# A hybrid conv block on one core: the first norm's squares shared by ScalarE and VectorE, its sum taken on TensorE in four parts, with zero matmuls between

## The chip, the cores and the metric

The kernel runs on one core of a Trainium2 chip. The metric is the device time of one execution in microseconds (us). A core has five queues that run side by side and wait for each other by semaphores: TensorE (PE, matmuls; its weight loads are shown as PEld), VectorE (DVE), ScalarE (ACT), GpSimd (POOL) and SyncE (SP, which here only issues DMAs).

## The reference

One layer on x of 1024 positions by 1024 channels, float32. A small vector c sets scales and shifts:

```python
mod = jax.nn.silu(c) @ w_ada[l] + b_ada[l]
sh1, sc1, g1, sh2, sc2, g2 = jnp.split(mod[:, None, :], N_MOD, axis=-1)
h = rms_norm(x, norm_mix_g[l]) * (1.0 + sc1) + sh1
proj = jnp.einsum('bsd,de->bse', h, w_in[l])
```

`rms_norm` divides by the root of the mean square over the channels. The projection feeds a short gated convolution and a 31-tap convolution module; their gated sum goes through one more matrix and is added to x; a second norm with its own modulation and a SwiGLU layer follow, then a last norm. The change touches only what comes before the first matmuls of `proj`: the squares, their sum, the root, and the first columns of `mod`.

## The kernel before, in words

Channels lie on the 128 partitions, positions along the free axis; 1024 channels are 8 chunks (k = 0 to 7), 1024 positions are 2 halves (h) of 512. A matmul multiplies a 128x128 block of weights with a 128x512 tile. Most products are made of float32r operands split in a high and a low part, so that one product is three matmuls: L286 (high weights, high operand), L287 (high weights, low operand), L289 (low weights, high operand), all in `mm3`. In the lead's first half, chunks 0 to 2 are multiplied whole in float32 instead (L282): the profile shows such a matmul as two records.

The lead is the part up to the end of the first seven columns of blocks of `proj` (`LEAD = 7`):

- SyncE loads x's first half as four tiles of two chunks (L442), then `ada` tiles (columns of w_ada, L266) and the weights `w_first` in the order of use. ScalarE's queue loads c and the vector of constants `vec`.
- c is spread over the partitions by two one-row matmuls (`cb`, L447); ScalarE's Silu of them is `cs` (L451).
- `squares_x` squares the eight chunks on ScalarE (L397) and adds them in a chain on VectorE (L401). `norm_start` sums over the partitions with one matmul by ones (`ss`, L407), and ScalarE takes an approximate reciprocal root (`rx0r`, L336). `rstd_end` sharpens it with three VectorE instructions, a Newton step (L341 to L343).
- `modulation(i)` makes one column of `mod` for one block of channels: a VectorE product of an `ada` tile with `cs`, summed along the row (L267). `affine` makes a scale from it (`aff`, L273).
- `modulate` multiplies a chunk with its scale and the norm (L353, VectorE); ScalarE adds the shift (L357, or L361 for a high part such as `h30h`: chunk 3, half 0), VectorE makes the low part (L362, `h30l`).
- `act_x(k, h)` calls these for a chunk and a half; `row_blocks` multiplies each chunk into seven PSUM tiles `lead`. In the second half (h = 1) the same is done with x's other half: its squares and their sum (`rx_1`) are made while chunks 6 and 7 of the first half are multiplied.
- Weights are split by a cast on ScalarE (`wh`, L208) and a subtraction on VectorE (`wl`, L209). There are three `wh` and three `wl` buffers, taken in turn, so a cast waits for the last matmul that reads the weights three casts earlier.
- `glu` and `gate` read the first half's seven `lead` tiles out of PSUM: ScalarE's Sigmoid (`sig`, L426 and L431) and VectorE's product (`u`, L427). The second half's tiles take the banks over as these come free.

The order on each queue is made by a scheduler from the code's order; `tc.issue_after(ins)` tells it to place what follows behind `ins`. After the lead come nine stages that the change does not touch.

Of the kernel before, what the change touches and what calls it, by code (L numbers as in the profile page):

```python
# [39 lines left out]
P = 128  # L40
# [7 lines left out]
CK = 31  # L48
# [62 lines left out]
def block_kernel(ctx: ExitStack, tc: tile.TileContext, x0, xT, c, vecs, ada, w_first, w_plain, w_duals,  # L111
# [35 lines left out]
    def hl_tile(name, dt=F32R):  # L147
        return tp.tile([P, H], dt, tag="t", name=name)
# [7 lines left out]
    def f32(t):  # L156
        return t.bitcast(F32)
# [102 lines left out]
    def modulation(i, raw=None):  # L260

        b = ADA_ORDER[i]
        if raw is None:
            raw = load(ada[i])
        else:
            nc.sync.dma_start(raw, ada[i])  # L266
        nc.vector.tensor_tensor_reduce(  # L267
            out=raw, in0=raw, in1=cs, scale=1.0, scalar=col(V_ADA, b),
            op0=ALU.mult, op1=ALU.add, accum_out=modc(b),
        )  # L270

    def affine(dst, k, sc, g):
        nc.vector.scalar_tensor_tensor(  # L273
# [119 lines left out]
    def squares_x(src, acc=None):  # L393

        for t in src:
            sq = g_tile("sq")
            act = nc.scalar.activation(sq, t, AF.Square, scale=1.0 / 32.0)  # L397
            if acc is None:
                acc = sq
            else:  # L400
                add = nc.vector.tensor_tensor(acc, acc, sq, ALU.add)  # L401
        squares_x.ins = act.ins, add.ins
        return acc
# [36 lines left out]
    for k in range(0, KC, 2):  # L440
        t = uc_tile("x0", T)
        nc.sync.dma_start(t, x0[k // 2])  # L442
        xin[k], xin[k + 1] = (t[:, s] for s in halves)
    cb = []
    for s in halves:
        cb.append(ps_tile("cb"))
        nc.tensor.matmul(cb[-1], ones[:1], crow[:, s], start=True, stop=True)  # L447
    acc = squares_x([xin[k] for k in range(KC)])
    with tc.issue_after(squares_x.ins[0]):
        for s, t in zip(halves, cb):  # L450
            silu = nc.scalar.activation(cs[:, s], t, AF.Silu)  # L451
    load_rsqrt(silu.ins)
    rx_0 = rstd_end(*norm_start(acc, "rx0"))

    def lead_w(k):
        if k < WHOLE:
# [3 lines left out]
    def act_x(k, h):  # L460
        nonlocal rx_1
        if h == 0:
            with ExitStack() as after:
                after.enter_context(tc.issue_after(modulate.ins[0] if k else squares_x.ins[1]))
                for i in range(2 * k, 2 * k + 2):
                    modulation(i, ucp.tile([P, T + CK - 1], F32, tag="uc", name="ada")[:, :D])
            affine(aff1, k, 8, V_GMIX)
            x[k, 0] = s_tile(f"x{k}0")
        whole = h == 0 and k < WHOLE
        hT[k][h] = modulate(x[k, h], rx_1 if h else rx_0, aff1[:, k : k + 1], modc(k),  # L470
                            None if whole else f"h{k}{h}", None if h else xin[k])
        if h == 0:
            if k == X1_AT:
                for i in range(KC):
                    x[i, 1] = s_tile(f"x{i}1")
                    nc.sync.dma_start(x[i, 1], xT[i, :, halves[1]])
            elif k == X1_AT + 1:
                with tc.issue_after(modulate.ins[2]):
                    rx_1 = squares_x([x[i, 1] for i in range(KC)])
                with tc.issue_after(mm3.ins), tc.issue_after(modulate.ins[1]):  # L480
                    rx_1 = norm_start(rx_1, "rx1", ss_tile=ps2_tile)
            elif k == KC - 1:
                with tc.issue_after(modulate.ins[2]):
                    rx_1 = rstd_end(*rx_1)
            if whole:
                return x[k, 0]
        elif k < WHOLE:
            hT[k][0] = split(x[k, 0], hl_tile, f"h{k}0")
        return hT[k][h]
# [733 lines left out]
```

## Time and profile before

| | |
|---|---|
| runs | 1496.49, 1498.00, 1498.34 us; median 1498.0 |
| profiled execution | 1498.83 us, of which the span of its instructions is 1497.1 |
| busy in the span | PE 1467.0, DVE 1140.8, ACT 623.8, POOL 537.7 us |
| first lead matmul (L282) | at 18.72 us |
| second half of the lead (L286 with h01h) | from 63.78 us |

Busy time is summed over the instructions of an engine. In the views, "a <-b" behind a time names what the engine waited for before it. Records of consecutive matmuls overlap by some 0.16 us, so their spacing, not their duration, is what one costs.

### The profile page before, as it was taken

To read this page: it belongs to the slowest core of one execution; us is meant where nothing else is said; L and a number is where in the kernel's file an instruction comes from. 1 tells how busy PE (TensorE), PEld (TensorE's weight loads), DVE (VectorE), ACT (ScalarE), POOL (GpSimd) and SP (SyncE) were. 2 spreads that over 40 slices of the span, in tenths; PEclk is the share of its full clock that TensorE was granted. 3 is DMA by queue.
4 is the path that set the end of the run, shared out by engine and by line. 5 is a ranking of instruction groups with operands and counts; after the bars stand their busy time and mean duration, and the time that the engine had idled before them with its cause. 6 is when DMAs were issued, how large, how long until landed. Compare 5 with 4: busy or idle time off the path is not lost.

```text
span 1497.1 us, 17720 instructions
## 1 busy us (share of the span) xinstructions
PE 1467.0 (98%) x6455; PEld 1201.2 (80%) x6455; DVE 1140.8 (76%) x1569; ACT 623.8 (42%) x896; POOL 537.7 (36%) x467
## 2 busy tenths in 40 slices
PE   6999999999999999999999999999999999999997
PEld 2788888888888788888788878888888888888887
DVE  7994999887887984767767699977666665677755
ACT  4653434343443353245335464544444443222235
POOL 0037777777767773410121001110000016545005
PEclk9999999999999999999999999999999999999999
DMA  9512223232222268455765437654444449998403
GB/s 352 208 65 70 99 71 113 70 99 85 99 71 85 99 248 314 148 185 167 245 203 165 140 113 267 231 167 150 149 148 154 151 151 356 362 313 263 134 28 113
DMA packets 83129, 248.82 MB, mean 166 GB/s; under 512 B 9569, under 2 KB 11745, under 8 KB 83042
## 3 DMA queue, kind: packets, MB, share of 16 engines
q1 hardware_dynamic: 42208, 139.48, 27.9%
q0 software_dynamic: 36944, 95.44, 19.4%
q10 hardware_dynamic: 3890, 12.78, 2.2%
q8 instruction: 50, 0.82, 0.2%
q14 instruction: 37, 0.30, 0.1%
HBM read 185.27 MB, written 62.39 MB: 165 GB/s over the span
## 4 chain that ended last, share of the span: by engine, by line
PE 91%; DVE 5%; issue 1%; DMA 1%; ACT 1%; POOL 0%; POOLq 0%; ACTq 0%; DVEq 0%
PE x L286 10%; PE x L289 10%; PE x L287 10%; PE z L286 7%; PE z L287 7%; PE z L289 7%; PE y L286 6%; PE y L289 6%; PE y L287 6%; PE ya L289 2%; PE ya L286 2%; PE ya L287 2%; PE mix L286 2%; PE mix L287 2%; PE mix L289 2%; PE yb L289 2%
## 5 line engine op out<-in xcount | busy, mean ns | idle before, releaser
L208 ACT CAST wh<-raw 128x1024 fp32r<-128x1024 f32 (+2 forms) x257 | 259.3, 1010 | 484.0 <-PE x L287 124.4
L209 POOL TENSOR_TENSOR wl<-raw,wh 128x1024 fp32r<-128x1024 f32 x92 | 227.5, 2474 | 131.0 <-ACT wh L208 127.2
L209 DVE TENSOR_TENSOR wl<-raw,wh 128x1024 fp32r<-128x1024 f32 (+2 forms) x165 | 188.2, 1141 | 65.2 <-ACT wh L208 62.4
L674 DVE SCALAR_TENSOR_TENSOR c<-diff,vec,c 128x512 f32<-128x512 f32 x248 | 178.6, 751 | 3.3
L942 POOL DMA_DIRECT2D hid<-stage x71 | 37.7, 532 | 354.2 <-DVE stage L326 353.5
L286 PE MATMUL x<-th,wh 128*128 128x512 f32 x240 | 93.4, 389 | 0.0
L289 PE MATMUL x<-th,wl 128*128 128x512 f32 x240 | 93.4, 389 | 0.0
L287 PE MATMUL x<-tl,wh 128*128 128x512 f32 x240 | 93.4, 389 | 0.0
L674 DVE SCALAR_TENSOR_TENSOR c<-u,wsum,c 128x512 f32<-128x512 f32 x112 | 84.1, 751 | 1.8
L267 DVE CUSTOM_DVE_ANT_0 raw<-raw,cs,vec 128x1024 f32<-128x1024 f32 x24 | 35.4, 1481 | 51.2 <-DMA raw<-in_ada 51.2
L286 PE MATMUL z<-th,wh 128*128 128x512 f32 x168 | 65.4, 389 | 0.0
L287 PE MATMUL z<-tl,wh 128*128 128x512 f32 x168 | 65.4, 389 | 0.0
L289 PE MATMUL z<-th,wl 128*128 128x512 f32 x168 | 65.4, 389 | 0.0
L231 POOL TENSOR_TENSOR raw<-raw 128x1024 f32<-128x1024 f32 x12 | 29.8, 2483 | 95.1 <-DVE wl L209 94.3
L325 ACT CAST stage<-g 128x512 fp32r<-128x512 f32 x62 | 38.3, 621 | 53.6 <-DMA hid<-stage 27.4
L326 DVE TENSOR_TENSOR stage<-g,stage 128x512 fp32r<-128x512 f32 x62 | 42.4, 687 | 20.8 <-ACT stage L325 20.7
L968 POOL DMA_DIRECT2D th<-hid x71 | 38.0, 535 | 50.9 <-PE x L289 28.5
L286 PE MATMUL yb<-zsh,wh 128*128 128x512 f32 x128 | 50.0, 391 | 3.5 <-DVE gb L796 3.5
L286 PEld LDWEIGHTS x<-th,wh 128*128 128x128 f32 x240 | 45.1, 188 | 9.5 <-issue 0.2
L289 PEld LDWEIGHTS x<-th,wl 128*128 128x128 f32 x240 | 45.1, 188 | 9.4
L287 PEld LDWEIGHTS x<-tl,wh 128*128 128x128 f32 x240 | 45.0, 188 | 9.3
L286 PE MATMUL y<-th,wh 128*128 128x512 f32 x132 | 51.3, 389 | 0.0
(1012 smaller groups left out, 4256.7 us busy)
## 6 DMA issues: line engine op xcount, KB each, us to landing
hid<-stage POOLq DMA_DIRECT2D x71, 512.0 KB, 4.5
raw<-in_w_fi SPq DMA_DIRECT2D x53, 512.0 KB, 4.2
raw<-in_w_duals SPq DMA_DIRECT2D x48, 512.0 KB, 3.5
th<-hid POOLq DMA_DIRECT2D x71, 256.0 KB, 5.7
tl<-hid POOLq DMA_DIRECT2D x71, 256.0 KB, 5.7
ada<-in_ada SPq DMA_DIRECT2D x24, 512.0 KB, 6.1
raw<-in_ada SPq DMA_DIRECT2D x24, 512.0 KB, 4.6
raw<-in_w_fo SPq DMA_DIRECT2D x24, 384.0 KB, 5.9
```

The costliest lines, as they stand in the source:

```text
L208: nc.scalar.copy(wh, raw)
L209: lo = lo_engine.tensor_tensor(wl, raw, f32(wh), ALU.subtract)
L231: eng.tensor_tensor(a["s1"], a["21"], a["22"], ALU.add)
L267: nc.vector.tensor_tensor_reduce(out=raw, in0=raw, in1=cs, scale=1.0, scalar=col(V_ADA, b), op0=ALU.mult, op1=ALU.add, accum_out=modc(b),)
L286: nc.tensor.matmul(ps, wh, xh, start=first, stop=False, skip_group_check=again)
L287: nc.tensor.matmul(ps, wh, xl, start=False, stop=False, skip_group_check=again)
L289: mm3.ins = nc.tensor.matmul(ps, wl, xh, start=False, stop=last, skip_group_check=again).ins
L325: nc.scalar.copy(hi, src)
L326: t_split.ins = nc.vector.tensor_tensor(lo, src, f32(hi), ALU.subtract).ins
L674: tap.ins = nc.vector.scalar_tensor_tensor(out=out, in0=src[:, s : s + H], scalar=wt, in1=acc, op0=ALU.mult, op1=ALU.add).ins
L942: nc.gpsimd.dma_start(hid_dram[key], s)
L968: nc.gpsimd.dma_start(t, hid_dram[key][:, s])
```

## The change

Four things, all in the lead:

1. Of each pair of chunks, ScalarE squares one and VectorE the other; VectorE adds the two, and TensorE sums the four pair sums over the partitions into one PSUM tile (`ss`), instead of one sum at the end of a chain.
2. A tile of zeros (`warm`, float32r) is filled on GpSimd; matmuls of it into a PSUM tile that nobody reads (`idle`) stand in TensorE's queue: three at the start, one behind each of the first three sums, twelve behind the fourth.
3. The two Silu of c stand between the squares on ScalarE.
4. The first two modulations (i = 0 and 1) are placed ahead of the Newton step.

```diff
-        nc.vector.tensor_tensor_reduce(
+        modulation.ins = nc.vector.tensor_tensor_reduce(
             out=raw, in0=raw, in1=cs, scale=1.0, scalar=col(V_ADA, b),
             op0=ALU.mult, op1=ALU.add, accum_out=modc(b),
-        )
+        ).ins
...
+    warm = hl_tile("warm")
+    nc.gpsimd.memset(f32(warm), 0.0)
+    idle = ps2_tile("idle")
+
+    def keep_warm(n):
+        for _ in range(n):
+            nc.tensor.matmul(idle, warm[:, :P], warm, start=True, stop=True)
+
+    keep_warm(3)
     cb = []
     for s in halves:
         cb.append(ps_tile("cb"))
         nc.tensor.matmul(cb[-1], ones[:1], crow[:, s], start=True, stop=True)
-    acc = squares_x([xin[k] for k in range(KC)])
-    with tc.issue_after(squares_x.ins[0]):
-        for s, t in zip(halves, cb):
-            silu = nc.scalar.activation(cs[:, s], t, AF.Silu)
-    load_rsqrt(silu.ins)
-    rx_0 = rstd_end(*norm_start(acc, "rx0"))
+    ss = ps_tile("ss")
+    for k in range(0, KC, 2):
+        sq = g_tile("sq"), g_tile("sq")
+        act = nc.scalar.activation(sq[0], xin[k], AF.Square, scale=1.0 / 32.0)
+        nc.vector.scalar_tensor_tensor(
+            out=sq[1], in0=xin[k + 1], scalar=1.0 / 1024.0, in1=xin[k + 1], op0=ALU.mult, op1=ALU.mult
+        )
+        last_sum = nc.vector.tensor_tensor(sq[0], sq[0], sq[1], ALU.add).ins
+        sums = nc.tensor.matmul(ss, ones, sq[0], start=k == 0, stop=k == KC - 2)
+        with tc.issue_after(sums.ins):
+            keep_warm(1 if k < KC - 2 else 12)
+        if k in (2, 4):
+            with tc.issue_after(act.ins):
+                nc.scalar.activation(cs[:, halves[k // 2 - 1]], cb[k // 2 - 1], AF.Silu)
+    load_rsqrt(act.ins)
+    rx_0 = rstd_start(ss, eps1, "rx0")
+    with tc.issue_after(last_sum):
+        for i in range(2):
+            modulation(i, uc_tile("ada", D))
+    with tc.issue_after(modulation.ins):
+        rx_0 = rstd_end(*rx_0)
...
         if h == 0:
-            with ExitStack() as after:
-                after.enter_context(tc.issue_after(modulate.ins[0] if k else squares_x.ins[1]))
-                for i in range(2 * k, 2 * k + 2):
-                    modulation(i, ucp.tile([P, T + CK - 1], F32, tag="uc", name="ada")[:, :D])
+            if k:
+                with tc.issue_after(modulate.ins[0]):
+                    for i in range(2 * k, 2 * k + 2):
+                        modulation(i, uc_tile("ada", D))
```

The scheduler also lays later parts of the lead otherwise. Behind the lead, all queues keep their order. Three places are shown. The changed kernel's lines above 444 have numbers of their own (L461 is the new square, L464 the new add, L465 the sum, L450 a zero matmul).

First, VectorE's queue from the constant `ngf` to the first modulate, of before (ISA is the modulation L267, with a row of its own for reading its sum out):

```order
L1017 TENSOR_SCALAR ngf<-vec 128x8 [waits DMAHW2_49]
L401 TENSOR_TENSOR sq<-sq 128x512 [waits Activation_49]
L401 TENSOR_TENSOR sq<-sq 128x512 [waits DVE_49,Activation_49] x6
L267 ISA ada,mod<-ada,cs,vec 128x1024 [waits DMAHW6_49,Activation_49]
L267 ISA mod 128x1
L267 ISA ada,mod<-ada,cs,vec 128x1024 [waits DMAHW7_49]
L273 SCALAR_TENSOR_TENSOR aff_104<-mod,vec 128x1 [waits DVE_49]
L341 SCALAR_TENSOR_TENSOR rx0t<-rx0r 128x512 [waits Activation_49]
```

and of the change, the first pair and then the end:

```order
L461 SCALAR_TENSOR_TENSOR sq<-x_128 128x512 [waits DMAHW1_49]
L1041 TENSOR_SCALAR ngf<-vec 128x8 [waits DMAHW2_49]
L464 TENSOR_TENSOR sq<-sq 128x512 [waits DVE_49,Activation_49]
L461 SCALAR_TENSOR_TENSOR sq<-x_130 128x512 [waits DMAHW3_49]
...
L267 ISA ada,mod<-ada,cs,vec 128x1024 [waits DMAHW6_49]
L273 SCALAR_TENSOR_TENSOR aff_104<-mod,vec 128x1 [waits DVE_49]
L267 ISA ada,mod<-ada,cs,vec 128x1024 [waits DMAHW7_49]
L341 SCALAR_TENSOR_TENSOR rx0t<-rx0r 128x512 [waits Activation_49]
```

The first square moved ahead of `ngf`, squares and adds alternate behind it, and the small `aff` moved between the two modulations.

Second, ScalarE's queue where the second half begins (`lead_175`, `177`, `179`, `181` and `lead_202`, `204`, `206`, `208` are the same four PSUM tiles of the first half; `x_337` and `x_358` are chunk 1 of the second). Before:

```order
L426 ACTIVATE sig<-lead_175 128x512 [waits PE_49]
L361 ACTIVATE h01h<-x_335,mod 128x512 [waits DVE_49]
L426 ACTIVATE sig<-lead_177 128x512 [waits PE_49]
L426 ACTIVATE sig<-lead_179 128x512 [waits PE_49]
L317 CAST h00h<-x_189 128x512
L365 ACTIVATE x_335<-x_335,mod 128x512 [waits DVE_49]
L208 CAST wh<-raw 128x896 [waits DMAHW0_49,PE_49]
L431 ACTIVATE sig<-lead_181 128x512 [waits PE_49]
L361 ACTIVATE h11h<-x_337,mod 128x512
```

With the change:

```order
L426 ACTIVATE sig<-lead_204 128x512 [waits PE_49]
L361 ACTIVATE h01h<-x_356,mod 128x512 [waits DVE_49]
L426 ACTIVATE sig<-lead_206 128x512 [waits PE_49]
L317 CAST h00h<-x_210 128x512
L365 ACTIVATE x_356<-x_356,mod 128x512 [waits DVE_49]
L208 CAST wh<-raw 128x896 [waits DMAHW0_49,PE_49]
L431 ACTIVATE sig<-lead_208 128x512 [waits PE_49]
L432 DMA gate_b_115<-sig 128x512 [waits Activation_49]
L208 CAST wh<-raw 128x896 [waits DMAHW1_49,PE_49]
L361 ACTIVATE h11h<-x_358,mod 128x512 [waits DVE_49]
```

A second cast moved ahead of `h11h`; two `sig` instead of one stand ahead of `h01h`. Farther up, the cast that waits on DMAHW7 moved ahead of the second half's root `rx1r`.

Third, VectorE's queue at the same place. Before:

```order
L353 SCALAR_TENSOR_TENSOR x_337<-x_337,aff_104,rx1r 128x512
L353 SCALAR_TENSOR_TENSOR x_339<-x_339,aff_104,rx1r 128x512
L427 TENSOR_TENSOR u_519<-lead_176,sig 128x512 [waits PE_49,Activation_49]
L362 SCALAR_TENSOR_TENSOR h01l<-x_335,mod,h01h 128x512 [waits Activation_49]
L209 TENSOR_TENSOR wl<-raw,wh 128x896 [waits DMAHW7_49]
L318 TENSOR_TENSOR h00l<-x_189,h00h 128x512 [waits Activation_49]
L427 TENSOR_TENSOR u_524<-lead_178,sig 128x512 [waits PE_49]
L209 TENSOR_TENSOR wl<-raw,wh 128x896 [waits DMAHW0_49,PE_49,Activation_49]
L427 TENSOR_TENSOR u_529<-lead_180,sig 128x512
L362 SCALAR_TENSOR_TENSOR h11l<-x_337,mod,h11h 128x512 [waits DVE_49,Activation_49]
```

With the change:

```order
L362 SCALAR_TENSOR_TENSOR h01l<-x_356,mod,h01h 128x512 [waits Activation_49]
L209 TENSOR_TENSOR wl<-raw,wh 128x896 [waits DMAHW7_49,PE_49]
L318 TENSOR_TENSOR h00l<-x_210,h00h 128x512 [waits Activation_49]
L427 TENSOR_TENSOR u_540<-lead_203,sig 128x512 [waits PE_49]
L209 TENSOR_TENSOR wl<-raw,wh 128x896 [waits DMAHW0_49,PE_49,Activation_49]
L427 TENSOR_TENSOR u_545<-lead_205,sig 128x512
L427 TENSOR_TENSOR u_550<-lead_207,sig 128x512
L353 SCALAR_TENSOR_TENSOR x_358<-x_358,aff_104,rx1r 128x512
L353 SCALAR_TENSOR_TENSOR x_360<-x_360,aff_104,rx1r 128x512
```

All three `u` now stand behind `h01l`, and the modulates of the next chunks behind them. On TensorE, the second half's sum `ss` (L407) moved from the middle of chunk 6 to its end, ahead of chunk 7, and the first three products of h01 now begin with their L286.

## The prediction

> **What bounds the kernel now.** I read the page's head, then who TensorE (PE) waited for, over the whole span (total us, times, longest).
>
> ```profile
> span 1497.1 us, 17720 instructions
> PE 1467.0 (98%) x6455; PEld 1201.2 (80%) x6455; DVE 1140.8 (76%) x1569; ACT 623.8 (42%) x896; POOL 537.7 (36%) x467
> ```
>
> ```profile
> PE ss L407 <- DVE sq L401: 6.1, 1, 6.1
> PE lead L282 <- ACT x L357: 4.6, 1, 4.6
> PE yb L286 <- DVE gb L796: 3.5, 2, 1.8
> PE z L286 <- ACT g L917: 3.2, 1, 3.2
> ```
>
> TensorE is the bound: 98% busy. Of its waits, the first two stand in the lead, which the change rewrites. The later ones are chains that start at TensorE's own results, so they move with it: what the lead gains or loses arrives at the end. Instructions outside the lead keep their order on all five queues, so the sum is made there alone. The timeline of the first 39 us shows what the lead waits for (columns: start, duration, then the instruction).
>
> ```profile
> 6.49 0.17 DVE L1017 TENSOR_SCALAR ngf<-vec 128x8 f32<-128x8 f32 x1 [5.46 <-DMA vec<-in_vecs]
> 6.57 5.47 DVE L401 TENSOR_TENSOR sq<-sq 128x512 f32<-128x512 f32 x7
> 11.95 1.28 DVE L267 CUSTOM_DVE_ANT_0 ada<-ada,cs,vec 128x1024 f32<-128x1024 f32 x1
> 13.15 1.28 DVE L267 CUSTOM_DVE_ANT_0 ada<-ada,cs,vec 128x1024 f32<-128x1024 f32 x1
> 14.36 0.15 DVE L273 SCALAR_TENSOR_TENSOR aff<-mod,vec 128x1 f32<-128x1 f32 x1
> 14.92 0.69 DVE L341 SCALAR_TENSOR_TENSOR rx0t<-rx0r 128x512 f32<-128x512 f32 x1 [0.40 <-ACT rx0r L336]
> 17.16 0.75 DVE L353 SCALAR_TENSOR_TENSOR x<-x,aff,rx0r 128x512 f32<-128x512 f32 x1
> ...
> 9.79 1.07 ACT L451 ACTIVATE cs<-cb 128x512 f32<-128x512 f32 x2
> 14.20 0.69 ACT L336 ACTIVATE rx0r<-ss,eps 128x512 f32<-128x512 f32 x1 [1.82 <-PE ss L407]
> ...
> 12.09 2.07 PE L407 MATMUL ss<-sq,ones 128*128 128x512 f32 x2 [6.08 <-DVE sq L401]
> 18.72 20.31 PE L282 MATMUL lead<-x,raw 128*128 128x512 f32 x42 [4.56 <-ACT x L357]
> ```
>
> Seven chained adds behind a VectorE (DVE) instruction that waits until 6.49 for a constant end at 12.04. Then come the sum over partitions (to 14.16), the reciprocal root (to 14.89), Newton's three steps from 14.92, the first modulate at 17.16, ScalarE (ACT), and the first lead matmul at 18.72. From L341 to that matmul are 3.80 us.
>
> A second thing costs time there: TensorE starts at half speed. The granted clock of the slices says full, but the durations do not.
>
> ```profile
> L282 PE MATMUL lead<-x,raw 128*128 128x512 f32 x6 | 4.9, 975 | 4.6 <-ACT x L357 4.6
> ```
>
> ```profile
> L282 PE MATMUL lead<-x,raw 128*128 128x512 f32 x36 | 15.9, 599 | 0.0
> ```
>
> ```profile
> 55.31 1.12 PE L407 MATMUL ss<-sq,ones 128*128 128x512 f32 x2
> ```
>
> A float32 matmul is two records. Those that start between 18 and 23 us last 975 ns, the other 36 last 599; the sum over partitions took 2.07 at 12.09 and 1.12 at 55.31. At 0.44 each (15.9 / 36) the 42 would take 18.5, not 20.31; with 0.43, the spacing of single records, 18.2. So half speed costs 1.8 to 2.1; I take **2.0**. Half a matmul then takes some 0.85.
>
> **The change part by part.** *Squares and adds.* VectorE now does four squares and four adds. One square runs before 6.49; seven operations stay behind the constant, as before. Their price is L341's 0.69 (two operands from SBUF) or at most the 0.75 of L353; I take 0.69. But only an add follows its own square and waits for it (0.79 apart, as the old adds); a square follows an add at 0.60 (below, 65.29 to 65.89). So the last add ends at 6.57 + 3 x 1.39 + 0.69 = 11.43, **0.6 earlier** than 12.04. ScalarE does four squares instead of eight, with the two Silu between them; they end near 8.6 instead of 10.86, while the first modulation needs them at 11.4: free.
>
> *First modulations.* They start at 11.4 instead of 11.95; with 1.20 each, and the small `aff` now between them (0.2), L341 cannot start before 14.05. That is 0.87 earlier than 14.92: the most that the norm can gain. Their two loads keep their place in SyncE's queue.
>
> *Four sums on TensorE.* Here the gain is lost. At half speed a sum takes 1.71 and the zero matmul behind it 0.43, together 2.14, while the pairs come every 1.39. From the first add's end at 7.3, all at half speed, the fourth sum would end at 7.3 + 0.2 + 4 x 1.71 + 3 x 0.43 + 0.2 = 15.8 (old: 14.16). At full speed it would follow the last add: 11.43 + 1.1 = 12.5, and the modulations would be the bound. The rate rises some 4.1 us after dense work begins (18.72 to about 22.8, where the short records begin); dense work now begins at 7.3, where a switch need not come after the same time. The slices and the timeline around 890 us show switches again.
>
> ```profile
> 889.00:891.00 2.00, 0.36 (x1) 0.36 (x2) 2.00 (x5) 2.00 (x5) 0.00 (x0) 0.70 0.81 256
> ...
> 895.00:897.00 2.00, 2.00 (x7) 1.55 (x6) 1.83 (x2) 0.00 (x0) 0.00 (x0) 0.59 0.70 287
> ```
>
> ```profile
> 887.10 0.39 PE L289 MATMUL x<-t3h,wl 128*128 128x512 f32 x1
> 890.64 0.80 PE L286 MATMUL z<-b22h,wh 128*128 128x512 f32 x1 [3.15 <-ACT g L917]
> ```
>
> The seventh column is the clock: 0.70 and 0.59 of a 2 us slice mean a fall to half at 889.8 and a return at 896.6. These are 6.8 us apart, and I read them as two steps of 3.4. Three such steps back from the rise at 22.8 lies 12.6, the first step's end after a full step of the new dense work. I take it for the rise. Then the fourth sum ends at 14.2, the root at 14.95, L341 starts at 15.0: **0.1 later** than before. Ends: 0.87 earlier, 1.6 later.
>
> [...]
>
> *Zero matmuls.* Their operand needs a fill on GpSimd; L162's fill now ends at 1.06, and the next costs what this row shows.
>
> ```profile
> L699 POOL MEMSET tot<- 128x512 f32 x2 | 1.1, 527 | 1.3 <-DVE tl L326 1.2
> ```
>
> So three of them run from 1.7 to 3.0 and delay the broadcast of c by some 0.8, to 6.8: hidden, since cs is needed at 11.4. The twelve run from 14.1, 0.23 each, to 16.8, while Newton runs; the lead starts at 15.0 + 3.8 = 18.8. If the rate holds over that gap of 2.0 us, the first 42 records take 18.2. **Gain: 2.0 - 0.1 = 1.9**, at the start of k = 3.
>
> *What is late next.* The scheduler has also laid the end of the first half otherwise. The rows of before there:
>
> ```profile
> 58.57 0.39 PE L287 MATMUL lead<-h60l,wh 128*128 128x512 f32 x1
> 59.02 0.39 PE L286 MATMUL lead<-h70h,wh 128*128 128x512 f32 x1
> 63.78 0.39 PE L286 MATMUL lead<-h01h,wh 128*128 128x512 f32 x1
> 68.66 0.40 PE L286 MATMUL lead<-h11h,wh 128*128 128x512 f32 x1
> ...
> 59.00 0.94 ACT L208 CAST wh<-raw 128x896 fp32r<-128x896 f32 x1 [1.23 <-PE lead L287]
> 59.95 1.28 ACT L426 ACT_TABLE_LOAD   x1
> 61.74 0.72 ACT L361 ACTIVATE h01h<-x,mod 128x512 fp32r<-128x512 f32 x1
> ...
> 63.03 0.74 DVE L362 SCALAR_TENSOR_TENSOR h01l<-x,mod,h01h 128x512 fp32r<-128x512 f32 x1
> 63.69 1.08 DVE L209 TENSOR_TENSOR wl<-raw,wh 128x896 fp32r<-128x896 f32 x1
> 64.69 0.68 DVE L318 TENSOR_TENSOR h00l<-x,h00h 128x512 fp32r<-128x512 f32 x1
> 65.29 0.68 DVE L427 TENSOR_TENSOR u<-lead,sig 128x512 f32<-128x512 f32 x1
> 65.89 1.08 DVE L209 TENSOR_TENSOR wl<-raw,wh 128x896 fp32r<-128x896 f32 x1
> 66.89 0.68 DVE L427 TENSOR_TENSOR u<-lead,sig 128x512 f32<-128x512 f32 x1
> ```
>
> Before, k = 7 began at 59.02, the second half (h01) at 63.78 and h11 at 68.66, almost without a wait. The second half's norm had its sum at 55.31, in the middle of k = 6. Now this sum stands behind k = 6, and its root behind a cast that needs a `wh` buffer. There are three of those, and a cast begins 0.04 after the last L287 of the products three casts back (58.57 + 0.39 to 59.00).
>
> k = 6 ends at 59.02 - 1.07 (the sum gone) - 1.9 = 56.05. The sum ends at 57.2, the root at 57.9, L341 starts at 57.95, the modulate (2.24 later, as at 14.92 to 17.16) at 60.2, h01h at 60.95 to 61.7, h01l behind a `wl` (1.0) at 61.85 to 62.6. TensorE does k = 7 from 57.0 to 61.8 (21 at 0.227), then three matmuls with h01h, and waits 0.15 for h01l. Behind h01l VectorE now runs, with the spacings of these rows, wl 62.5, h00l 63.5, u 64.1, wl 64.7, u 65.7 (done 66.4), u 66.3. Each `u` frees a PSUM bank for h01; before, the first stood ahead of h01l. TensorE wants the first at 64.7 and waits 0.1, the second at 65.5 and waits **0.9**; the third is there. Its last L287 ends at 67.75.
>
> Then the clear loss: on ScalarE the cast that waits for exactly this L287 now stands ahead of h11h; before, h11h came first. Cast from 67.75, h11h from 68.6 to 69.3 (0.94 and 0.72, overlapping by 0.1), matmul at 69.35, where TensorE would have gone on at 67.8: **1.55**. So h11 starts at 69.35 instead of 68.66: **+0.7**. By then h11l (ready at 70.3, wanted at 70.7) and all later operands are ahead of their matmuls, as they were before.
>
> The profiled execution took 1498.83 (span 1497.1 and 1.7 around it), so the sum gives 1499.5 for it. The median of the runs, 1498.0, lies 0.8 below; their spread of 1.9 is of a size that other places of the clock's switches could make. Put on the median: **1498.7**.
>
> **The rivals.** *The reordered waits are hidden.* If h11h and the `u` came in time, 1.9 would stay: 1496.1. For it speaks that before nothing waited there; against it, that the cast needs the L287 that TensorE runs last. 15%.
>
> *The rate falls back in the gap* behind the twelve zero matmuls. The rows at 887 show a fall 2.3 us after the last record's end (887.49 to 889.8) with a pause of 3.15; the new gap is 2.0. A fall there makes one step of 3.4 run at half speed, +1.7: 1500.4. [...] 20%.
>
> *Zero matmuls do not raise the rate*, so the change does not do what it says, and ends slower. For it speaks that the broadcast of c, 3.75 us of one-row matmuls from 2.26, raised nothing. Then the fourth sum ends at 15.8, L341 starts at 16.5, the twelve end at 15.6 + 5.1 = 20.7, and the lead starts there, 2.0 late and cold as before. k = 6 ends at 59.95, h11 starts at 73.3, +4.6: 1502.6. It decides as soon as the records of the four sums all last a microsecond. 12%.
>
> **How the numbers follow.** The forecast has 50%, the rivals 15, 20 and 12, and 3% is spread beyond. The range runs from the first rival, 1496.0, to 1501.5: past the second with some place of the switches added. It leaves out the third and the tails, together under 2 in 10. About 0.2%, 3 us, is what a measurement of this kernel can tell from no change. Under 1495.0: 4%. Over 1501.0: the third rival and the upper edge of the second, 15%. Between: 81%.
>
> **What would show it.** Right: lead matmuls of about 600 ns from the first; L341 between 14.05 and 16; ScalarE waiting for PE at a cast just ahead of h11h, and TensorE waiting 1.5 us for h11h and 0.9 for a `u`. Wrong: no wait at h11 (first rival), records of 1 us in the lead (second), or in all sums (third). A new wait outside the lead would break the premise that the lead's balance reaches the end.

## The result and the profile after

The changed kernel takes **1501.72 us** (median of 14 runs, 1497.98 to 1504.36); the kernel before took 1498.15 beside it (14 runs, 1496.23 to 1499.13). The ratio is 1.0022, 95% interval 1.0015 to 1.0030: slower by 2.2 to 4.5 us. (The ratios here compare all the runs of two kernels and differ a little from the quotient of the medians.) A second measurement of the same kernel (below) gave 1.0009 (1.0000 to 1.0017). Two measurements of one kernel thus lie 0.0013 apart, some 2 us, and smaller differences between kernels say little by themselves. The profiled execution took 1502.65 us, 3.82 more than the one of before.

The head of the page after, and who TensorE waited for over the whole span (total us, times, longest):

```profile
span 1500.9 us, 17764 instructions
...
PE 1476.6 (98%) x6479; PEld 1206.4 (80%) x6479; DVE 1141.3 (76%) x1570; ACT 621.6 (41%) x892; POOL 537.9 (36%) x468
```

```profile
PE yb L286 <- DVE gb L820: 4.5, 2, 3.3
PE z L286 <- ACT g L941: 3.2, 1, 3.2
PE lead L282 <- ACT x L357: 1.8, 1, 1.8
PE idle L450 <- POOL warm L445: 1.6, 1, 1.6
PE lead L286 <- ACT h11h L361: 1.4, 1, 1.4
```

Of before's two waits in the lead, the one of 6.1 us is gone and the one of 4.6 has become 1.8, because the zero matmuls fill the rest. One of 1.4 us is new in the second half (h11h). And one outside the lead has grown: yb for gb, 4.5 instead of 3.5, the longest 3.3 instead of 1.8. The change touches nothing there. (The 1.6 is the start: the first zero matmuls wait for the fill on GpSimd.)

The time moved in three places: ahead of the lead, in the second half, and in the yb stage. First matmul of each, in us:

| | before | after | difference |
|---|---|---|---|
| first lead matmul (L282) | 18.72 | 18.61 | -0.11 |
| k = 3 (h30h) | 38.46 | 38.03 | -0.43 |
| second half, chunk 1 (h11h) | 68.66 | 70.89 | +2.23 |
| second half, chunk 2 (h21h) | 73.43 | 75.77 | +2.34 |
| yb | 662.98 | 665.30 | +2.32 |
| mix, the stage after yb | 754.10 | 759.05 | +4.95 |
| last stage (y<-th) | 1440.32 | 1444.15 | +3.83 |

Between mix and the last stage 1.1 us come back: around 890 us TensorE waits 3.2 us in both (z for `g`), and the rate then fell for 6.8 us in before (889.79 to 896.62), for 3.4 in after (896.03 to 899.45).

**Ahead of the lead** all went as laid out up to its first matmul. The timeline (start, duration, instruction, what it waited for):

```profile
10.91 0.69 DVE L464 TENSOR_TENSOR sq<-sq 128x512 f32<-128x512 f32 x1
...
11.90 1.06 PE L465 MATMUL ss<-sq,ones 128*128 128x512 f32 x2
...
12.92 1.28 DVE L267 CUSTOM_DVE_ANT_0 ada<-ada,cs,vec 128x1024 f32<-128x1024 f32 x1
13.03 1.02 PE L465 MATMUL ss<-sq,ones 128*128 128x512 f32 x2
...
13.49 3.31 PE L450 MATMUL idle<-warm 128*128 128x512 f32 x12
...
14.81 0.69 DVE L341 SCALAR_TENSOR_TENSOR rx0t<-rx0r 128x512 f32<-128x512 f32 x1 [0.60 <-ACT rx0r L336]
...
18.61 5.83 PE L282 MATMUL lead<-x,raw 128*128 128x512 f32 x9 [1.81 <-ACT x L357]
```

The last add ends at 11.60, the fourth sum at 14.05, the zero matmuls at 16.80, and the lead starts after 1.81 us of idling. In its first records the rate is half again. The lead's matmuls between 18 and 23 us, in number, busy us and mean ns, and then two windows (length, busy time of PE and four other engines, the clock in the seventh column):

```profile
L282 PE MATMUL lead<-x,raw 128*128 128x512 f32 x7 | 5.0, 875 | 1.8 <-ACT x L357 1.8
```

```profile
15.40:18.81 3.41, 1.60 (x8) 1.02 (x7) 3.31 (x5) 0.72 (x1) 0.00 (x0) 1.00 0.98 391
18.81:22.22 3.41, 3.41 (x5) 1.35 (x5) 3.37 (x8) 0.72 (x1) 0.00 (x0) 0.50 0.66 204
```

The trace's records of the clock have it full from 11.98, half from 18.81 to 22.22, and full again. The three times lie on one grid of 3.413 us, and so do all later switches of that execution (721.95 is 208 steps behind 11.98). The step that ended at 18.81 had TensorE busy for 1.60 of 3.41 us.

**In the second half**, timeline of ScalarE, VectorE and TensorE:

```profile
67.07 1.28 DVE L427 TENSOR_TENSOR u<-lead,sig 128x512 f32<-128x512 f32 x2
...
68.27 2.73 DVE L353 SCALAR_TENSOR_TENSOR x<-x,aff,rx1r 128x512 f32<-128x512 f32 x4
...
69.27 0.94 ACT L208 CAST wh<-raw 128x896 fp32r<-128x896 f32 x1 [3.24 <-PE lead L287]
...
70.11 0.72 ACT L361 ACTIVATE h11h<-x,mod 128x512 fp32r<-128x512 f32 x1
...
70.89 1.65 PE L286 MATMUL lead<-h11h,wh 128*128 128x512 f32 x6 [1.42 <-ACT h11h L361]
```

The cast waits for TensorE's L287, h11h stands behind the cast, and TensorE waits 1.42 for h11h. From h30h to h21h it takes 37.74 us; before, 34.97.

**In the yb stage**, the same three instructions after and before:

```profile
714.46 0.50 PE L286 MATMUL yb<-zsh,wh 128*128 128x512 f32 x1 [1.17 <-DVE gb L820]
...
720.27 0.69 DVE L820 TENSOR_TENSOR gb<-yb,gb 128x512 f32<-128x512 f32 x1 [3.46 <-DMA gb<-gate_b]
...
721.02 0.50 PE L286 MATMUL yb<-zsh,wh 128*128 128x512 f32 x1 [3.30 <-DVE gb L820]
```

```profile
712.78 0.50 PE L286 MATMUL yb<-zsh,wh 128*128 128x512 f32 x1 [1.81 <-DVE gb L796]
...
716.94 0.69 DVE L796 TENSOR_TENSOR gb<-yb,gb 128x512 f32<-128x512 f32 x1 [1.81 <-DMA gb<-gate_b]
...
717.69 0.50 PE L286 MATMUL yb<-zsh,wh 128*128 128x512 f32 x1 [1.67 <-DVE gb L796]
```

VectorE waits for a load of 256 KB (gb<-gate_b), TensorE for VectorE, since `gb` frees the bank. Counted from the issue, that load took 6.08 us after and 4.43 before. Behind the longer wait the rate fell too (half from 721.95 to 725.36; before, it stayed full here). What else moved from 714 to 721 us, by DMA queue (packets, MB, share) and by load (count, size, median us to landing), after:

```profile
q1 hardware_dynamic: 247, 0.88, 32.7%
q0 software_dynamic: 239, 0.79, 32.5%
q8 instruction: 1, 0.02, 0.9%
issues: line engine op xcount, KB each, median us to landing
gb<-gate_b POOLq DMA_DIRECT2D x3, 256.0 KB, 5.5
```

One packet of the kind "instruction", 16 KB, which I read as a piece of program. In the same stretch of before (712 to 719) there is none, though the other queues moved no less, and its four loads took 4.0 in the median:

```profile
q1 hardware_dynamic: 272, 0.98, 39.3%
q0 software_dynamic: 240, 0.79, 31.5%
...
gb<-gate_b POOLq DMA_DIRECT2D x4, 256.0 KB, 4.0
```

Over the whole execution this queue moves 51 such pieces, 0.84 MB (before 50, 0.82 MB), one per 127 of TensorE's 6479 matmuls with their weight loads (in before one per 129 of 6455). If they are TensorE's program, the zero matmuls and the three added sums, 24 records more, move the places at which it is fetched. Here the piece comes 52.7 us after yb's first matmul; before, 57.1. The load's 16 parts say how it may hurt: 15 had landed at 52.8 in that count, the last at 54.9; in before all 16 came between 52.7 and 53.9. That the late part stood behind the piece the trace does not say; c1 and c2 below test it.

This gave three theories, with rivals, for the runs: the **order** of the second half costs 2.8 us (rival: the zero matmuls themselves do); the **rate** falls back in the idle stretch ahead of the lead, in some executions (rival: always, or zero matmuls don't raise it at all); the **piece of program** meets the load at yb (rivals: chance, or the earlier lead).

### The profile page after: what moved, and what is told of

Its sections match the earlier page's. It is cut to its first block, busy times and chain, and to the rows that moved or that the text cites. A ratio compares the mean times of both kernels' runs of the same rounds, so it can differ in the third digit from the quotient of the medians.

```text
span 1500.9 us, 17764 instructions
## 1 busy us (share of the span) xinstructions
PE 1476.6 (98%) x6479; PEld 1206.4 (80%) x6479; DVE 1141.3 (76%) x1570; ACT 621.6 (41%) x892; POOL 537.9 (36%) x468
## 4 chain that ended last, share of the span: by engine, by line
PE 91%; DVE 5%; ACT 1%; issue 1%; DMA 1%; POOL 0%; POOLq 0%; ACTq 0%; DVEq 0%
PE x L286 10%; PE x L289 10%; PE x L287 10%; PE z L286 7%; PE z L289 7%; PE z L287 7%; PE y L286 6%; PE y L289 6%; PE y L287 6%; PE ya L286 2%; PE ya L287 2%; PE ya L289 2%; PE mix L286 2%; PE mix L287 2%; PE yb L286 2%; PE yb L289 2%
## 5 line engine op out<-in xcount | busy, mean ns | idle before, releaser
L966 POOL DMA_DIRECT2D hid<-stage x71 | 37.8, 533 | 353.7 <-DVE stage L326 353.0
L286 PE MATMUL x<-th,wh 128*128 128x512 f32 x240 | 93.4, 389 | 0.0
L287 PE MATMUL x<-tl,wh 128*128 128x512 f32 x240 | 93.4, 389 | 0.0
L267 DVE CUSTOM_DVE_ANT_0 raw<-raw,cs,vec 128x1024 f32<-128x1024 f32 x24 | 34.6, 1447 | 51.7 <-DMA raw<-in_ada 51.7
L286 PE MATMUL z<-th,wh 128*128 128x512 f32 x168 | 65.4, 389 | 0.0
L287 PE MATMUL z<-tl,wh 128*128 128x512 f32 x168 | 65.4, 389 | 0.0
L325 ACT CAST stage<-g 128x512 fp32r<-128x512 f32 x62 | 38.3, 621 | 49.1 <-DVE g L955 22.7
L286 PE MATMUL yb<-zsh,wh 128*128 128x512 f32 x128 | 50.8, 397 | 4.5 <-DVE gb L820 4.5
L287 PEld LDWEIGHTS x<-tl,wh 128*128 128x128 f32 x240 | 45.1, 188 | 9.3
L286 PEld LDWEIGHTS x<-th,wh 128*128 128x128 f32 x240 | 45.0, 188 | 9.3
L289 PE MATMUL y<-th,wl 128*128 128x512 f32 x132 | 51.3, 389 | 0.0
```

Of the source, the lines that this page charges most:

```text
L267: modulation.ins = nc.vector.tensor_tensor_reduce(out=raw, in0=raw, in1=cs, scale=1.0, scalar=col(V_ADA, b), op0=ALU.mult, op1=ALU.add, ac ...
L286: nc.tensor.matmul(ps, wh, xh, start=first, stop=False, skip_group_check=again)
L287: nc.tensor.matmul(ps, wh, xl, start=False, stop=False, skip_group_check=again)
L289: mm3.ins = nc.tensor.matmul(ps, wl, xh, start=False, stop=last, skip_group_check=again).ins
L325: nc.scalar.copy(hi, src)
L966: nc.gpsimd.dma_start(hid_dram[key], s)
```

## The experiments

All twelve were timed in 11 runs each beside the kernel before on the same chip: 33 runs of before (median 1498.82) for the first four, 32 (1498.97) for the next four, 27 (1499.05) for three, 15 (1498.44) for the last. What their profiles say, and those of before and after (all but the median is of one profiled execution each):

| | h30h at | h30h to h21h | piece, after yb's start | load of gate_b | yb to mix | median |
|---|---|---|---|---|---|---|
| before | 38.46 | 34.97 | 57.1 | 4.43 | 91.12 | 1498.15 |
| before, again (b3) | 38.29 | 34.99 | 57.9 | 4.30 | 92.55 | 1499.06 |
| before + zero matmuls (b2) | 36.20 | 37.77 | 46.5 | 4.35 | 90.68 | 1498.76 |
| before + tiny matmuls (c1) | 38.28 | 35.08 | 52.6 | 5.73 | 93.63 | 1500.17 |
| after | 38.03 | 37.74 | 52.7 | 6.08 | 93.75 | 1501.72 |
| after, again (a1) | 36.83 | 37.78 | 52.4 | 5.91 | 93.62 | 1500.94 |
| twenty zero matmuls (a2) | 35.79 | 37.78 | 53.0 | 5.97 | 92.68 | 1500.18 |
| one cast behind (a3) | 37.16 | 36.66 | 52.6 | 4.19 | 91.14 | 1499.15 |
| three casts, twenty (b1) | 36.71 | 36.68 | 51.6 | 5.29 | 91.15 | 1499.88 |
| three casts, twelve (b4) | 35.91 | 36.69 | 52.0 | 4.97 | 93.25 | 1500.84 |
| after + tiny matmuls (c2) | 36.04 | 37.77 | 38.3 | 4.32 | 91.38 | 1498.18 |
| no zero matmuls (a4) | 38.71 | 34.88 | 55.7 | 4.76 | 91.12 | 1497.50 |
| no zero matmuls, again (c3) | 37.67 | 34.85 | 55.9 | 4.64 | 92.91 | 1498.71 |
| all three mends (d1) | 36.78 | 36.69 | 38.6 | 4.47 | 91.73 | 1497.80 |

The stretch from yb to mix adds up in all fourteen profiles: 87.4 to 87.8 us, plus TensorE's idle time there (2.1 to 4.5, nearly all for gb), plus 1.7 where a step of 3.41 us ran at half rate. Such steps move the time of a run too. Of the 107 runs of before beside the experiments, the 47 with a mean granted clock of 0.996 average 1499.5 us, the 36 with 0.997 1498.3 and the 17 with 0.998 1497.6.

**a1: the changed kernel again.** No edit.

> The changed kernel as it is, profiled a second time. Theory (the rate falls back in the 2.0 us gap behind the twelve zero matmuls whenever one step of the clock's counter holds most of the gap, and the second half's new order costs 2.7 us): the second half loses the same 2.7 us between the first matmul of chunk 3 and the first with h21h; the start of the lead shows records of 1.06 us only if a step happens to hold the gap, else 0.59 from the first. The wait of the yb products for gate_b's load, 3.3 us against 1.8 before, comes back if the shift made it, and varies if it is chance. Rival (the fall is always there): L282 starts with five long records again. Time near 1501.7 on either.

Measured: 1500.94 us, ratio 1.0009 (1.0000 to 1.0017). The rate held ahead of the lead this time. Two steps of this execution's grid:

```profile
13.06:16.47 3.41, 3.41 (x13) 2.26 (x12) 2.20 (x4) 0.69 (x1) 0.00 (x0) 1.00 1.02 416
16.47:19.89 3.42, 1.63 (x6) 0.86 (x5) 3.35 (x6) 0.72 (x1) 0.00 (x0) 1.00 0.71 283
```

No lead record is long, and h30h comes at 36.83 instead of 38.03. So the fall is a matter of the execution: the idle stretch was 1.8 us in both, with 1.60 busy us in its step the rate fell, with 1.63 it held. That is no sharp line: with twelve zero matmuls again, it held with 1.59 in a3. Over all fourteen profiles the steps behind which the rate fell had at most 1.60 us of work, those behind which it held at least 1.51. The second half (37.78) and yb (load 5.91) are as in the first profile.

**a2: twenty zero matmuls.** Behind the fourth sum, to fill the idle stretch.

```diff
-            keep_warm(1 if k < KC - 2 else 12)
+            keep_warm(1 if k < KC - 2 else 20)
```

> Twenty zero matmuls behind the fourth sum instead of twelve: at 0.227 us each they reach to about 0.2 us ahead of the first lead matmul, so no step of the counter can hold an idle gap; all queues keep their order. Theory (fall in the gap costs 1.7 when it comes): no long L282 record in any profile, first h21h matmul near 74.1 us against 75.8, median 1 to 1.7 us under the changed kernel's in the same rounds. Rival (zero matmuls do not hold the rate, only real ones do): long records stay and the time stays.

Measured: 1500.18 us, ratio 1.0010 (1.0001 to 1.0019). The lead starts at 18.06 without idling, and h30h at 35.79, 2.67 earlier than before. At h21h 0.14 is left on the wrong side. So the fall ahead of the lead is not what made the median slow.

**a3: one cast behind h11h.** The cast of the second half's fourth weights is placed behind h11h, as it stood before.

```diff
-    ... weights(w_first[k], LEAD * P, [modulate.ins[2 if k else 0]]) ...
+    ... weights(w_first[k], LEAD * P, ([modulate.ins[1]] if k == 3 else []) + [modulate.ins[2 if k else 0]]) ...
```

> One added rule of order: the cast of the second half's fourth weights stands behind h11h on ScalarE, as in the kernel before. Theory (that cast ahead of h11h costs 1.4 to 1.55): TensorE's wait for h11h falls from 1.4 us to under 0.3, the wait for a u (0.6) stays, and the second half loses 1.3 us instead of 2.7 between the first matmul of chunk 3 and the first with h21h; time 1.4 under the changed kernel. Rival (VectorE's late modulate of chunk 1 is the real bound): the wait for h11h stays over 1 us and is then put down to the modulate.

Measured: 1499.15 us, ratio 1.0000 (0.9992 to 1.0009). TensorE's waits between 55 and 76 us:

```profile
PE lead L286 <- DVE u L427: 0.6, 1, 0.6
PE lead L286 <- ACT h11h L361: 0.3, 1, 0.3
```

The wait for h11h falls from 1.4 to 0.3, the stretch from 37.8 to 36.7: this one cast costs 1.1 of the 2.8. Here the piece of program came at 52.6 and yet the load took 4.19: a meeting need not hold it up.

**a4: no zero matmul at all.**

```diff
-    keep_warm(3)
...
-        with tc.issue_after(sums.ins):
-            keep_warm(1 if k < KC - 2 else 12)
```

> The change without any zero matmul: shared squares, four pair sums, the first modulations ahead of Newton. The scheduler then leaves the second half nearly as in the kernel before (h11h ahead of the cast, its sum inside chunk 6). Theory: the sums run at half rate, the fourth ends near 14.7 us, Newton starts near 15.4, the lead near 19.2 with four to eight long records, and the second half loses under 0.5 us: time within 1.0 us of the kernel before, 2 to 3 us under the changed kernel. Rival (the shared squares themselves cost the 3 us): time near 1501.7.

Measured: 1497.50 us, ratio 0.9992 (0.9983 to 1.0001). The four sums alone raise the rate (13.25), it falls back while TensorE idles 4.6 us, and the lead begins at half rate: h30h at 38.71, no gain. But the scheduler lays the second half nearly as before, 34.88, and the piece comes at 55.7, behind the parts that count.

**b1: twenty zero matmuls, three casts put back.** Those of the second half's weights 1, 2 and 3 go behind rx1r, h00h and h11h, as before.

```diff
+    def behind(k):
+        return rx_act if k == 1 else [split.hi] if k == 2 else [modulate.ins[1]] if k == 3 else []
...
-    ... [modulate.ins[2 if k else 0]]) ...
+    ... behind(k) + [modulate.ins[2 if k else 0]]) ...
```

> The changed kernel with twenty zero matmuls behind the fourth sum instead of twelve, and with three casts of the second half's lead put back by hand to where they stood before: that of the weights of k = 1 behind the reciprocal square root of the second half, that of k = 2 behind the cast h00h, that of k = 3 behind h11h. If the second half's loss is the order of ScalarE's and VectorE's work there, the stretch from h30h to h21h takes 35.0 +/- 0.3 us as before (34.97; 37.8 in the changed kernel), and what the rate gains in the lead (h30h at 35.8 to 37.2 against 38.46) reaches the end: 1.3 to 2.7 us faster than before, about 1496.5. Rival: the zero matmuls themselves delay the second half (the rate, the banks): the stretch stays near 37.8 and the time stays at 1500. Second rival, for yb: the load of gate_b takes 6 us and the rate falls there whenever the lead is early or carries zero matmuls; then 1.3 to 2 us are lost again at yb, and the time is 1498.

Measured: 1499.88 us, ratio 1.0009 (1.0000 to 1.0018). Wrong on both counts: the stretch took 36.68, no better than with one cast, and the load at yb took 5.29. ScalarE's casts are not the whole order. Timeline of the last kernel below (d1), whose second half is the same to 0.01 us:

```profile
64.22 0.68 DVE L427 TENSOR_TENSOR u<-lead,sig 128x512 f32<-128x512 f32 x1
...
65.82 1.28 DVE L427 TENSOR_TENSOR u<-lead,sig 128x512 f32<-128x512 f32 x2
...
66.56 0.50 PE L286 MATMUL lead<-h01h,wh 128*128 128x512 f32 x1 [0.64 <-DVE u L427]
...
67.02 2.06 DVE L353 SCALAR_TENSOR_TENSOR x<-x,aff,rx1r 128x512 f32<-128x512 f32 x3
...
67.79 0.72 ACT L361 ACTIVATE h11h<-x,mod 128x512 fp32r<-128x512 f32 x1 [3.01 <-DVE x L353]
```

h11h now waits for its modulate (L353), which VectorE has placed behind the three `u`; before, VectorE did two such modulates at 61.10 and 61.77, ahead of them. This points to VectorE's order for the remaining 1.7 us. That order was put back in no run with zero matmuls, so it is not shown, and the split of the 1.7 stays open. The tile `idle` alone is not the cause: c1 below has it too, with matmuls into it, and its stretch is 35.08.

**b2: the kernel before with zero matmuls alone.** Three at the start, fourteen around cb, eighteen behind the sum; the chain of squares and the place of the modulations stay.

```diff
+    keep_warm(3)
     cb = []
...
+    keep_warm(14)
     acc = squares_x([xin[k] for k in range(KC)])
...
+    with tc.issue_after(norm_start.ins):
+        keep_warm(18)
```

> The kernel before, its chain of eight squares and seven adds and its Newton steps kept, with zero matmuls alone added: three at the start, fourteen around the two matmuls of cb, eighteen behind the matmul of the sum. If zero matmuls raise the rate, the records shorten by 16.1 at the latest, the eighteen are done before 18.7, the lead starts where it did (18.7) and has no long record: h30h at 36.5 against 38.46. The list's new order in the second half then takes 2.8 away again: h21h at 74.2 against 73.43, the time 1499 to 1499.6. Rival (zero matmuls do not raise the rate): the eighteen last until 22, the lead starts there at the low rate, h30h at 41.5, and the time is above 1503.

Measured: 1498.76 us, ratio 1.0002 (0.9993 to 1.0011). The lead's records, shortest, median and longest in ns, with first and last start, and the waits between 55 and 76 us:

```profile
L282 PE MATMUL lead<-x,raw x42: 592/592/697, 18.5 to 36.2; 128*128 128x512 f32 x42
```

```profile
PE lead L286 <- ACT h11h L361: 1.4, 1, 1.4
PE lead L286 <- DVE u L427: 0.6, 1, 0.6
```

Zero matmuls raised the rate: it rose at 12.52, at the end of a step of 3.41 us that held nothing else (8.14 to 12.94), and no lead record is long. They alone also make the second half's order: the same two waits, the same 37.77. The gain at h30h, 2.26, is gone at h21h (+0.54).

**b3: the kernel before, again.** No edit.

> The kernel before, unchanged. If the length of the load of gate_b ahead of yb (4.4 or 6.0 us) and the fall of the rate there are a matter of one execution, this profile may show either; if they come with the change, it shows 4.4 us and no fall, as before. The time says how far two copies of one kernel lie apart: within 0.7 us of each other.

Measured: 1499.06 us, ratio 0.9998 (0.9989 to 1.0007). The load took 4.30, as in the first profile; the rate fell at yb (714.97 to 718.38) behind a wait of 2.9. So that fall comes without the change too, and the load's length, alike in the two profiles, goes with the program.

**b4: as b1, with twelve zero matmuls.**

> As the kernel with twenty and the three casts put back, but with the twelve zero matmuls of the changed kernel, so that TensorE idles 2 us ahead of the lead. If the rate holds over that gap, h30h stands at 36 to 37.2 and the time equals that with twenty (within 0.5 us); if it falls back, as in the first profile of the changed kernel and not in the second, h30h stands at 38 and the profiled time is 1.5 us later. The stretch from h30h to h21h takes 35.0 in both.

Measured: 1500.84 us, ratio 1.0009 (0.9999 to 1.0019). The rate held over the idle stretch in this profile, h30h at 35.91; load 4.97, a fall at yb. Of the five profiles with twelve zero matmuls, one fell ahead of the lead.

**c1: the kernel before with twelve tiny matmuls.** They stand ahead of cb, where TensorE waits for c; no other instruction on any queue changes its place. Only TensorE's program is 24 matmuls and 24 weight loads longer, as in the changed kernel.

```diff
+    idle = ps2_tile("idle")
+    for _ in range(12):
+        nc.tensor.matmul(idle[:1, :8], ones[:, :1], ones[:, :8], start=True, stop=True)
     cb = []
```

> The kernel before with twelve tiny float32 matmuls (1 x 8, of ones, result unused) ahead of the matmuls of cb, where TensorE waits for c anyway: 24 matmuls and 24 weight loads more in its program, nothing else changed, every later instruction of every engine in the same order. TensorE's program comes in pieces of 16 KB, one per about 128 matmuls with their weight loads; in before the piece in the yb stage is fetched 57.1 and 57.9 us after yb begins, in three profiles with the changed kernel's program 52.4 to 53.0, in the middle of the loads of gate_b whose last part then lands 5.9 to 6.1 us after the issue instead of 4.3 to 4.4. If that fetch is what holds the load up, it moves here to 52 to 53.5, the load takes 5.3 to 6.1, TensorE waits 1 us longer for gb (4.5 instead of 3.5), and the time is 0.5 to 2 us above before. Rival (the load's length goes with the changed lead, or is chance): the load takes 4.4 and the time equals before within 0.7. The lead itself should stand as before: h30h 38.3 to 39.

Measured: 1500.17 us, ratio 1.0004 (0.9995 to 1.0013). The piece moved from 57.1 to 52.6, and yb became that of the changed kernel, its load 5.73. The rows, and the stretch's DMA:

```profile
717.85 0.69 DVE L799 TENSOR_TENSOR gb<-yb,gb 128x512 f32<-128x512 f32 x1 [3.11 <-DMA gb<-gate_b]
...
718.60 0.79 PE L286 MATMUL yb<-zsh,wh 128*128 128x512 f32 x1 [2.92 <-DVE gb L799]
```

```profile
q8 instruction: 1, 0.02, 0.9%
issues: line engine op xcount, KB each, median us to landing
gb<-gate_b POOLq DMA_DIRECT2D x3, 256.0 KB, 5.1
```

The parts of the load came as in after: 15 by 53.4, the last at 54.9. The lead is untouched (h21h 73.36), so the longer load needs no earlier lead. From yb to mix the profile has 2.5 us more than before: some 1.0 is the wait for gb (4.5 against 3.5), 1.7 a half-rate step. Against b3, which had such a step too, it is 1.1. In the time, the median is 1.1 us up and the ratio stands for 0.6, which its interval does not tell from nothing.

**c2: the changed kernel with twenty tiny matmuls** at the very start, ahead of its three zero matmuls; everything behind them in the same order.

> The changed kernel with twenty tiny float32 matmuls (1 x 8, result unused) at the very start: 40 matmuls and 40 weight loads more in TensorE's program, the order of everything else unchanged. The piece of program that was fetched at 52.4 to 53.0 us of the yb stage is then fetched near 44, ahead of the loads of gate_b that TensorE waits for. If the fetch is the cause, that load takes 4.2 to 4.5, TensorE's wait for gb falls from 4.5 to 3.5, the rate falls less often there, and the time is 0.7 to 2 us below the changed kernel, near 1499.5. Rival: the load stays at 6 and the time at 1501. The lead and its second half stand as in the changed kernel: h21h 74 to 76.

Measured: 1498.18 us, ratio 1.0001 (0.9992 to 1.0011). The piece comes at 38.3 (44 was expected), none in the stretch; the load takes 4.32:

```profile
717.54 0.69 DVE L822 TENSOR_TENSOR gb<-yb,gb 128x512 f32<-128x512 f32 x1 [1.70 <-DMA gb<-gate_b]
```

With twenty matmuls whose results nobody uses, the median of the changed kernel is 2.8 and 3.5 us below its two measurements, though its second half still takes 37.77. By the ratios it is 1.2 and 3.1 us, and the interval overlaps that of a1: the load's length is shown to go with the piece, the size of the gain in the time is not.

**c3: no zero matmul, again** (a4's kernel).

> The changed kernel without any zero matmul, a second time. With the second half in the order of before, and TensorE's program only 6 matmuls longer than before (its piece fetched at 55.7, behind the parts that TensorE waits for), nothing that costs the changed kernel is left; the first time it was 1.3 us below before, interval 0.9983 to 1.0001. If that gain is real, the ratio is 0.9985 to 0.9995 again; if it was chance, 1.000.

Measured: 1498.71 us, ratio 0.9992 (0.9982 to 1.0001), the same as the first time. Each interval alone touches 1; two alike speak for a gain of 1.2 us. The window of TensorE's idling, one grid step, ends with the fall:

```profile
14.87:18.29 3.42, 0.04 (x1) 0.04 (x1) 3.31 (x5) 0.72 (x1) 0.00 (x0) 1.00 0.98 331
18.29:21.70 3.41, 3.41 (x4) 1.45 (x5) 3.37 (x7) 0.72 (x1) 0.00 (x0) 0.50 0.89 300
```

**d1: all three mends.** Twenty zero matmuls (a2), one cast behind h11h (a3), twenty tiny matmuls (c2).

> The changed kernel with all three mends: twenty zero matmuls behind the fourth sum, so that the rate holds up to the lead; the cast of the second half's fourth weights behind h11h; twenty tiny matmuls at the start, so that TensorE's piece of program is fetched ahead of the loads of gate_b that it waits for. If lead, second half and fetch are all that separates the kernels: h30h at 35.8 to 37.2, h21h at 72.5 to 73.5, the load of gate_b 4.2 to 4.5 us, and a time 0.5 to 1.5 us below before, the level of the kernel without zero matmuls (ratio 0.999 to 0.9997). If VectorE's pace holds the second half, as in the run with three casts put back, h21h stays at 73.4 and the time equals before (1.000).

Measured: 1497.80 us, ratio 0.9998 (0.9989 to 1.0007). The lead is fast (h30h 36.78), at yb the load takes 4.47 and the rate holds (TensorE still waits 4.0 for gb, before 3.5), and h21h stands at 73.47, where before has 73.43: the second half takes back all that the lead gains.

## Why the prediction came out as it did

- *Last add 0.6 earlier, at 11.43*: 11.60. **Held.**
- *First modulations free, L341 not before 14.05*: the second one ends at 14.20, L341 waits 0.60 for the root. **Held.**
- *The four sums lose the gain; rate up at 12.6; L341 at 15.0*: up at 11.98, L341 at 14.81. In the nine other profiles with four sums the rate rose between 11.03 and 13.64, so 12.6 was near the middle of what they show. It was worked out from the grid of another execution, whose place is its own: that it came within 0.6 is luck. That a rise ends a step full of work was an estimate from before's rows; here too the step ahead of the rise (8.57 to 11.98) held 3.41 us of work. **Held**, L341 within 0.2.
- *Twelve zero matmuls to 16.8, lead at 18.8, the rate holds, gain 1.9 at k = 3*: 16.80 and 18.61. The rate held in four of the five profiles with twelve (gain at h30h 1.3 to 2.6) and fell in the first (0.43). The rival that the rate falls back was given 20% as one of several outcomes; it is a thing that happens in some executions of one kernel, and belonged into the forecast as a share of its 1.7. **Right as to kind.**
- *What is late next*: from h30h to h11h the prediction has 32.8 (69.35 less 36.56); measured 32.86, with 1.42 for h11h (1.55 predicted) and 0.64 for `u` (0.9). **Held**; at h21h the order costs 2.77.
- *Zero matmuls do not raise the rate* (12%): refuted by b2.
- *The reordered waits are hidden* (15%): refuted; both stand in every profile that has the order.
- *"Instructions outside the lead keep their order on all five queues, so the sum is made there alone"*: **the step that failed.** The order was kept; the number of TensorE's instructions was not, and with it moved the places at which the pieces of 16 KB come (c1: 57.1 to 52.6 us after yb's start). One of them met the load that yb waits for. Seven profiles have the piece at 51.6 to 53.0. In six of them the load took 5.0 us or more; they average 93.0 us from yb to mix (92.7 with a3, the seventh), the seven with the piece elsewhere 91.6. Their medians are 1499.9 to 1501.7 (a3 1499.2) against 1497.5 to 1499.1. So the term left out is some 1.4 us in the stage. Of it 0.8 is TensorE's wait, 4.1 on average against 3.3, and the rest the rate, which fell in five of the six and in three of the seven (b3, c2, c3); that it falls more often with the piece is not shown by so few. Nor does a longer load always make a longer wait: a2 and b1 waited 3.5, as before, with loads of 5.97 and 5.29. In the time, c1 against before has 0.6 us by the ratio (interval -0.7 to 1.9) and a1 against c2 1.2, so there the term's size stays open. That TensorE waits for gb at yb stood in the rows that the prediction quoted; that VectorE in turn waits there for a DMA (1.81 us in before) had no place in the sum. A new wait outside the lead was what the prediction itself named as breaking its premise: this one is an old wait that grew, from 3.5 to 4.5.

By its own steps the lead gave +0.7 us at h11h; in a1, where the rate held, it was +1.05. With the missing 1.4 of yb that is 2.1 to 2.5, and in some executions 1.7 more for the rate. Measured were +1.3 and +3.3 us by the two ratios (1.0009 and 1.0022), forecast +0.7 (1498.7 on 1498.0). The median of 1501.72 lies 0.2 above the range, that of a1 inside it; the first ratio on the forecast's base of 1498.0 gives 1501.3. That the time came so near the upper end is no merit of the sum: that end stood for the second rival, and yb had no term.

Open: how much of the second half's 1.7 is VectorE's order; why the load in a3 took 4.19 with the piece in its way; which of the falls of the rate around 890 us (3.4 or 6.8 us long, none in d1) are chance; and whether 1.2 us without zero matmuls is real.

## What to carry to other kernels

A change that keeps every order can still move time elsewhere, if it changes how many instructions a queue has (in c1, with 24 matmuls more and every order kept, the load took 5.73 us instead of 4.43 and TensorE waited 4.5 for gb instead of 3.5): look for DMA packets of the kind "instruction" beside loads that somebody waits for, and shift them with a few idle instructions to test it. A gain on the busiest engine reaches the end only as far as the next operands are early: read how long each was ready ahead of its first use (before, h01l was ready 0.24 us early: 63.03 + 0.74 against 64.01). And instructions that compute nothing are seen by the scheduler, which may lay out the next 50 us otherwise because of them (b2: 37.77 us from h30h to h21h instead of 34.97).

## What the runs showed of the hardware

- The clock's switches of one execution lay on a grid of 3.413 us (after: 11.98, 18.81, 22.22 and 721.95, 208 steps behind the first) whose place differed between executions (before had a switch at 22.81). After a pause of 1.8 us the rate fell where the step that held it had 1.60 us of work (after), and did not with 1.63 (a1) and 1.59 (a3). What makes the grid, a counter as the expectations call it or something else, no trace shows.
- Matmuls of zeros raised the rate (b2: at 12.52, behind a step that held nothing else). The one-row matmuls of cb did not: in before they ran from 2.26 to 6.01 and filled the step from 2.33 to 5.74, and the rate rose first at 22.81.
- A piece of 16 KB of the kind "instruction" took 0.96 us to move (after, at 718.04); with one beside it, a load in 16 parts had its last part late: 15 by 52.8 us, the sixteenth at 54.9 (after; c1 53.4 and 54.9). Moved away, the load took 4.32 (c2). In a3 a piece at the same place did no harm.
